# A decoder layer's expert stage: one-hots loaded once for each token, fewer tiles beside the selection

## The chip, the cores and the metric

The kernel runs on 1 core of one Trainium2 chip. The metric is the device time of one execution, in microseconds (us). The engines of a core each run their own list of instructions in order: PE (TensorE: matmuls; PEld is its weight loads), DVE (VectorE), ACT (ScalarE), POOL (GpSimd) and SP (SyncE, which here issues most transfers).

## The reference

One decoder layer for 256 tokens of width 1024: retention and attention heads between two projections, then a retrieval of single-neuron experts (PEER), then a norm. The change lies in the retrieval alone:

```python
def _peer(h, w_q, subkeys, w_down, w_up):      # 16384 experts, 8 heads, top 16, in blocks of 128 tokens
    q = (hblk @ w_q).reshape(B, TB, 8, 2, 128)
    s = einsum('btphd,phnd->btphn', q, subkeys)
    v, i = top_k(s, 16)                        # 16 of 128 for each half key
    cand = v[..., 0, :, None] + v[..., 1, None, :]
    cidx = i[..., 0, :, None] * 128 + i[..., 1, None, :]
    tv, tj = top_k(cand, 16)
    eidx = take_along_axis(cidx, tj, -1); w = softmax(tv)
    a = gelu(einsum('btd,btpkd->btpk', hblk, w_down[eidx]))
    return einsum('btpk,btpkd->btd', w * a, w_up[eidx])
```

## The kernel before

For 192 of the 256 tokens the experts aren't gathered: the hidden vectors are multiplied with all 16384 rows of `w_down` (128 **down units** of 128 experts, 512 KB each), gelu is taken, the result is multiplied by a weight matrix that is zero except at the chosen experts, and then multiplied with all of `w_up` (128 **up units**). For the other 64 tokens the chosen rows are gathered: 64 **sparse steps** for `w_down` (a gather of 512 KB on POOL, then a multiply with a sum on DVE: tile `row`, `dotS`) and 64 for `w_up` (`accS`).

A down unit comes in two forms. A *whole* unit multiplies the tile as loaded, in float32 (8 matmuls, each of which stands in the trace as two instructions of 192 columns: `acc<-h2f,raw`, `dn<-h2f,raw`). A *split* unit needs the tile cut into two fp32r parts (`H` on ACT, `L` on DVE, both 128x1024), takes 8 matmuls of 384 and 8 of 192 columns (`<-hT,H`, `<-hT,L`), and its two halves are added afterwards (`g` on ACT, then `g<-g,acc` on DVE). Up units are always split, and their gate values too (`a`).

The expert stage has three phases, kept by a loop over a list `seq` of units:

- **top**: after 16 query units, down units run on PE while DVE chooses the experts (`top_gen`, `top16`), for the first 128 tokens and then for the other 128. Each half ends with an exponential on ACT (`ex`, which needs an ACT table load before it and another after it), sums on DVE and three transposes on PE (`w<-ident,ef`, `w<-ident,ex`) that make the tables for the next phase. All down units of this phase are whole.
- **w**: `w_gen` builds the weight matrix in 48 groups of 4 tokens beside further down units. In a group DVE makes two one-hot tiles (`o1`, `o0`) and the high half of the weighted one-hot (`ow`), ACT the low half (`ow`, one instruction for each token), and PE multiplies them into one bank of PSUM: two loads of the same one-hot and two matmuls of 128 columns for each token. From the bank DVE multiplies into those parts of `VL`/`VH` whose down unit is already done, and ACT copies the others. Every third down unit is whole (`WD`).
- **up**: the remaining down units alternate with up units, then up units alone.

`credit` sets how many steps of `top_gen` or `w_gen` go with each unit: a unit adds `CT` in the phase top and `CD` in the phase w, and a step takes what it yields. `scred` does the same for sparse steps: `RD` for each unit, `RU` for each up unit. This list gives the order in which the instructions are written; a scheduler then orders them on DVE, ACT, PE and POOL, and `issue_after` keeps an instruction behind another one. SP issues loads in the written order. PSUM has 8 banks in this stage: 4 with the name `acc`, 2 `dn`, 2 `w`. Nearly all instructions of the trace carry line L88, a recording helper; so one goes by the tiles' names.

Of the kernel before, what the change touches and what calls it, by code (L numbers as in the profile page):

```python
# [24 lines left out]
F32 = mybir.dt.float32  # L25
# [11 lines left out]
P = 128  # L37
# [17 lines left out]
NJ = P // 2  # L55
BLK = 8
BD = 3
WD = 3
RD = 0.7
RU = 0.45  # L60
EARLY = 5
NF1 = 3
NF2 = 1
FAFTER = False
SPL = 1
CT = 1.1
AFTER = ("top",)
NCAND = 50
CAND = [(0, 0, 1, 16), (16, 1, 2, 8), (24, 2, 3, 5), (29, 3, 4, 4), (33, 4, 5, 3), (36, 5, 8, 2), (42, 8, 16, 1)]
# [2 lines left out]
def build(tc, I, out, dbg=None, stop=None):  # L72
# [868 lines left out]
    def top_gen(sc):  # L941

        for i in range(16):
            while i not in sc:
                yield None
            b = sc.pop(i)
            for tt in range(2):
                top16(b[:, tt, :], tv1[tt][:, i, :], ti1[tt][:, i, :], P, "s2")
                yield 1.1
        for tt in range(2):  # L950
            fi = mk(tk, (P, 8, 2, 16), F32, "fi", bufs=2)
            V.tensor_copy(fi, ti1[tt].rearrange("p (a b) c -> p a b c", b=2))
            V.tensor_scalar(fi[:, :, 0, :], fi[:, :, 0, :], 128.0, None, op0=ALU.mult)
            v4 = tv1[tt].rearrange("p (a b) c -> p a b c", b=2)
            cand = mk(tk, (P, 8, NCAND), F32, "cand", bufs=2)
            cidx = mk(tk, (P, 8, NCAND), F32, "cidx", bufs=2)
            for src, dst in ((v4, cand), (fi, cidx)):
                for o, a0, a1, nb in CAND:
                    n = (a1 - a0) * nb
                    V.tensor_tensor(dst[:, :, o:o + n].rearrange("p h (a b) -> p h a b", b=nb),  # L960
                                    src[:, :, 0, a0:a1, None].to_broadcast([P, 8, a1 - a0, nb]),
                                    src[:, :, 1, None, 0:nb].to_broadcast([P, 8, a1 - a0, nb]), op=ALU.add)
                yield 1.1
            tv = mk(tk, (P, 8, 16), F32, "tv", bufs=2)
            tp = mk(tk, (P, 8, 16), U32, "tp", bufs=2)
            tpf = mk(tk, (P, 8, 16), BF, "tpf", bufs=2)
            ev = mk(tk, (P, 8, 16), F32, "ev", bufs=2)
            for p in range(8):
                top16(cand[:, p, :], tv[:, p, :], tp[:, p, :], NCAND, "s3")
                V.tensor_copy(tpf[:, p, :], tp[:, p, :])  # L970
                oh = mk(tk, (P, NCAND, 16), BF, "oh", bufs=1)
                V.tensor_tensor(oh, ioj, tpf[:, p:p + 1, :].to_broadcast([P, NCAND, 16]), op=ALU.is_equal)
                oe = mk(tk, (P, NCAND, 16), F32, "oe", bufs=2)
                V.tensor_tensor(oe, oh, cidx[:, p, :, None].to_broadcast([P, NCAND, 16]), op=ALU.mult)
                V.tensor_reduce(ev[:, p, :], oe.rearrange("p j k -> p k j"), axis=AX.X, op=ALU.add)
                yield 2.1

            ex = mk(tk, (P, 8, 16), F32, "ex", bufs=2)
            V.tensor_tensor(ex, tv, tv[:, :, 0:1].to_broadcast([P, 8, 16]), op=ALU.subtract)
            S.activation(ex, ex, AF.Exp)  # L980
            sm = mk(tk, (P, 8), F32, "smx", bufs=2)
            V.tensor_reduce(sm, ex, axis=AX.X, op=ALU.add)
            V.reciprocal(sm, sm)
            V.tensor_tensor(ex, ex, sm[:, :, None].to_broadcast([P, 8, 16]), op=ALU.mult)
            ei = mk(tk, (P, P), I32, "ei", bufs=2)
            V.tensor_copy(ei, ev.rearrange("p a b -> p (a b)"))
            e1 = mk(tk, (P, 2, P), I32, "e1", bufs=1)
            V.tensor_scalar(e1[:, 0, :], ei, 7, None, op0=ALU.arith_shift_right)
            V.tensor_scalar(e1[:, 1, :], ei, 127, None, op0=ALU.bitwise_and)
            ef = mk(tk, (P, 2, P), F32, "ef", bufs=1)  # L990
            V.tensor_copy(ef, e1)
            if tt == 0:

                ew = ex.rearrange("p a b -> p (a b)")
                V.tensor_copy(idxS[:TS, :], ei[:TS, :NJ])
                V.tensor_copy(wS[:TS, :], ew[:TS, :NJ])
                G.dma_start(idxS[TS:, :], ei[:TS, NJ:])
                last["G"] = G.dma_start(wS[TS:, :], ew[:TS, NJ:])
                spg.append(sparse_gen())
            yield 1.3  # L1000
            b = bank("w")[:, :3 * P].rearrange("p (a b) -> p a b", a=3)
            PE.transpose(b[:, 0, :], ef[:, 0, :], ident)
            PE.transpose(b[:, 1, :], ef[:, 1, :], ident)
            PE.transpose(b[:, 2, :], ex.rearrange("p a b -> p (a b)"), ident)
            tq = slice(tt * P, (tt + 1) * P)
            S.activation(tab[:, :, tq], b[:, 0:2, :], AF.Copy)
            wt = mk(tk, (P, P), F32, "wt", bufs=1)
            S.activation(wt, b[:, 2, :], AF.Copy, scale=WSC)
            dump(f"e{tt}", ev)
            dump(f"w{tt}", ex)  # L1010

            V.tensor_copy(tabw[:, tq], wt)
            V.tensor_tensor(tabl[:, tq], wt, tabw[:, tq], op=ALU.subtract)
            yield 1.0
# [50 lines left out]
    def w_gen(ohp):  # L1065

        half = NT // 2
        for gi in range(TD // 4):
            v0 = gi * 4
            t0 = TS + v0  # L1070
            oh = []
            for n in (1, 0):
                o = mk(ohp, (P, P, WG), F16, f"o{n}")
                V.tensor_tensor(o, iow, tab[:, n, None, t0:t0 + WG].to_broadcast([P, P, WG]), op=ALU.is_equal)
                oh.append(o)
            ow = [mk(ohp, (P, P, WG), F16, f"ow{n}") for n in range(2)]
            V.tensor_tensor(ow[0], oh[1], tabw[:, None, t0:t0 + WG].to_broadcast([P, P, WG]), op=ALU.mult)
            for t in range(WG):
                S.activation(ow[1][:, :, t], oh[1][:, :, t], AF.Copy, scale=tabl[:, t0 + t:t0 + t + 1])
            b = bank("w").rearrange("p (a b) -> p a b", a=4)  # L1080
            for t in range(WG):
                for n in range(2):
                    mm(b[:, t, :], oh[0][:, :, t], ow[n][:, :, t], n == 0, n == 1)
            yield 1.0
            bv = b.rearrange("p t i -> p i t")
            na = state["na"]
            for i0, buf in ((0, VL), (half, VH[0])):
                a = min(max(na - i0, 0), half)
                o = buf[:, :, v0:v0 + 4]
                if a:  # L1090
                    V.scalar_tensor_tensor(o[:, :a, :], bv[:, i0:i0 + a, :], 1.0 / WSC, o[:, :a, :], op0=ALU.mult,
                                           op1=ALU.mult)
                if a < half:
                    S.activation(o[:, a:, :], bv[:, i0 + a:i0 + half, :], AF.Copy, scale=1.0 / WSC)
            state["t0"] = v0 + 4
            yield 0.4

    def down_unit(n):
        wide = n not in whole
        if wide:  # L1100
            h, l = splits.pop(("down", n))
        else:
            r, _ = raws.pop(("down", n))
        b = bank("dn" if phase == "up" or n % 3 == 2 else "acc")[:, :2 * TD]
        for k in range(KC):
            ks = slice(k * P, (k + 1) * P)
            if wide:
                two = [(b.rearrange("p (a b) -> p a b", a=2), h[:, ks], h2[k // 4][:, k % 4, :, TS:]),
                       (b[:, :TD], l[:, ks], h2H[:, k, TS:])]
                for n_, o in enumerate(two[::-1] if k else two):  # L1110
                    mm(*o, k == 0 and n_ == 0, k == KC - 1 and n_ == 1)
            else:
                mm(b[:, :TD], r[:, ks], h2f[:, k, :], k == 0, k == KC - 1)
        t0 = state["t0"]
        v = vtile(n)
        if t0 or wide:
            g = mk(gt, (P, TD), F32, "g")
        src = b
        if wide:
            S.activation(g, b[:, TD:], AF.Copy)  # L1120
            V.tensor_tensor(g, g, b[:, :TD], op=ALU.add)
            src = g
        if t0 < TD:
            last["U"] = S.activation(v[:, t0:], src[:, t0:TD], AF.Gelu_apprx_tanh)
        if t0:
            S.activation(g[:, :t0], src[:, :t0], AF.Gelu_apprx_tanh)
            last["U"] = V.tensor_tensor(v[:, :t0], v[:, :t0], g[:, :t0], op=ALU.mult)
        state["na"] = n + 1
# [100 lines left out]
    def split_to(i):  # L1229
        while splitted[0] <= i and splitted[0] < len(seq):  # L1230
            u, n = seq[splitted[0]]
            if u == "down" and (phase == "top" or phase == "w" and n % WD == 0):
                whole.add(n)
                splitted[0] += 1
                continue
# [245 lines left out]
```

## Time and profile before

| | us |
|---|---|
| median of 3 runs (966.09 to 971.69) | 967.46 |
| the profiled execution | 963.1 |
| its span | 960.9 |
| PE busy | 905.5 (94%) |
| DVE busy | 810.4 (84%) |
| ACT busy | 521.2 (54%) |
| POOL busy | 224.8 (23%) |

Matmuls overlap in the pipeline, so the busy time of PE says little of its speed; the distance from one unit's start to the next one's start does. In the program's span the first group of the phase w starts at 375.1 us, the last group ends at 570.0, the first up unit starts at 581.6, the last down unit at 682.1, and the last matmul ends at 948.2. The chain of waits lies 51% on PE, 26% on DVE, 8% on DMA and 7% on ACT.

### The profile page before, as it was taken

Reading aid. Unit: us, or ns where it says so; the run is one execution under the profiler, and the core shown is the slowest. Engines: PE = TensorE matmul, PEld = TensorE weight load, DVE = VectorE, ACT = ScalarE, POOL = GpSimd, SP = SyncE. Lnnn points to the kernel's source line nnn. Section 1 sums busy time; section 2 is a strip of 40 time slices with the busy share of each in tenths; the row PEclk is TensorE's granted clock in tenths of the full one; section 3 lists DMA queues with packets and bytes.
Section 4 is the critical chain, followed back from the end, with each engine's and each line's share of the span. In section 5 each row is a group of like instructions: output and inputs, shape, how many; then the busy total and the mean of one; then the engine's idle time right before and its main releaser. Section 6 shows DMA issues by size and latency. Waiting matters only on the chain.

```text
span 960.9 us, 15265 instructions
## 1 busy us (share of the span) xinstructions
PE 905.5 (94%) x5198; PEld 797.2 (83%) x5198; DVE 810.4 (84%) x1788; ACT 521.2 (54%) x1151; POOL 224.8 (23%) x172
## 2 busy tenths in 40 slices
PE   7999999999999799999989987899999989999994
PEld 6875667899999799999989986788887867888883
DVE  7988888689998922899998986889988979898887
ACT  7543697344221123778776754556564545555564
POOL 2040000110004200123223312334442425233311
PEclk9999999999999899999999988999999999999998
DMA  9978765354569976778777677899999999899981
GB/s 361 393 283 290 263 220 177 129 158 143 153 207 387 338 227 218 260 264 281 270 257 263 248 255 258 288 321 345 348 351 359 384 352 354 339 337 341 332 290 44
DMA packets 74749, 266.43 MB, mean 277 GB/s; under 512 B 9400, under 2 KB 9712, under 8 KB 74288
## 3 DMA queue, kind: packets, MB, share of 16 engines
q1 hardware_dynamic: 55200, 193.59, 57.5%
q0 software_dynamic: 19328, 71.61, 20.4%
q8 instruction: 41, 0.67, 0.3%
q14 instruction: 36, 0.29, 0.1%
q10 hardware_dynamic: 144, 0.26, 0.1%
HBM read 263.03 MB, written 2.11 MB: 276 GB/s over the span
## 4 chain that ended last, share of the span: by engine, by line
PE 51%; DVE 26%; DMA 8%; ACT 7%; issue 6%; POOL 1%; SPq 0%; DVEq 0%; ACTq 0%; POOLq 0%
PE acc L88 32%; DVE row L88 5%; PE C L88 5%; PE dn L88 4%; PE O L88 4%; DVE L L88 4%; PE S L88 3%; PE T L88 2%; DVE ev L88 2%; DVE o L88 2%; DMA row<-in_downN_dram,idxS 2%; ACT H L88 2%; ACT ow L88 1%; DMA raw<-in_down_dram 1%; DVE VL L88 1%
## 5 line engine op out<-in xcount | busy, mean ns | idle before, releaser
L88 DVE TENSOR_TENSOR L<-raw,H 128x1024 fp32r<-128x1024 f32 x216 | 263.2, 1220 | 41.9 <-ACT H L88 37.3
L88 ACT ACTIVATE H<-raw 128x1024 fp32r<-128x1024 f32 x216 | 228.2, 1058 | 122.2 <-DMA raw<-in_up_dram 73.4
L88 PE MATMUL acc<-H,a 128*128 128x512 f32 (+1 forms) x774 | 269.9, 397 | 4.4 <-DVE a L88 4.3
L88 PE MATMUL acc<-L,a 128*128 128x512 f32 (+1 forms) x515 | 203.4, 395 | 6.7 <-DVE L L88 6.7
L88 PEld LDWEIGHTS acc<-H,a 128*128 128x128 f32 x774 | 149.4, 193 | 39.8 <-DVE a L88 9.6
L1025 POOL DMA_INDIRECT row<-in_up_dram,idxS x64 | 116.2, 1815 | 196.2 <-DVE accS L88 163.8
L88 PE MATMUL acc<-h2f,raw 128*128 128x192 f32 x816 | 139.2, 326 | 0.0
L1025 POOL DMA_INDIRECT row<-in_downN_dram,idxS x64 | 77.5, 1210 | 242.6 <-DVE VH L88 85.4
L88 PEld LDWEIGHTS acc<-h2f,raw 128*128 128x128 f32 x816 | 133.0, 190 | 0.0
L88 PEld LDWEIGHTS acc<-L,a 128*128 128x128 f32 x515 | 99.1, 192 | 26.5 <-DVE L L88 7.1
L88 PE MATMUL dn<-hT,H 128*128 128x384 f32 x328 | 101.8, 367 | 5.4 <-DVE g L88 5.2
L88 PE MATMUL acc<-hT,H 128*128 128x256 f32 (+1 forms) x408 | 98.0, 323 | 3.6 <-ACT g L88 3.6
L88 DVE SCALAR_TENSOR_TENSOR row<-row,h2rep 128x1024 f32<-128x1024 f32 x64 | 77.9, 1218 | 8.8 <-DMA row<-in_downN_dram,idxS 8.6
L88 DVE SCALAR_TENSOR_TENSOR accS<-row,cS,accS 128x1024 f32<-128x1024 f32 x64 | 81.7, 1277 | 2.2 <-DMA row<-in_up_dram,idxS 2.2
L88 PE MATMUL dn<-hT,L 128*128 128x192 f32 x328 | 77.1, 255 | 0.0
L88 ACT ACTIVATE ow<-o,VL 128x128 f16<-128x128 f16 x192 | 74.4, 572 | 4.0 <-DVE o L88 3.4
L88 PEld LDWEIGHTS acc<-hT,H 128*128 128x128 f32 x408 | 69.7, 194 | 3.9 <-ACT g L88 3.9
L88 PE MATMUL acc<-hT,L 128*128 128x192 f32 (+1 forms) x280 | 72.5, 270 | 0.0
L88 PEld LDWEIGHTS dn<-hT,H 128*128 128x128 f32 x328 | 62.5, 191 | 8.5 <-DVE g L88 7.3
L88 PEld LDWEIGHTS dn<-hT,L 128*128 128x128 f32 x328 | 62.8, 193 | 0.7
L88 PE MATMUL w<-ow,o 128*128 128x128 f16 x384 | 53.2, 296 | 4.1 <-DVE ow L88 2.5
L88 PE MATMUL dn<-h2f,raw 128*128 128x192 f32 x272 | 48.5, 333 | 6.3 <-ACT VL L88 6.3
(355 smaller groups left out, 1367.2 us busy)
## 6 DMA issues: line engine op xcount, KB each, us to landing
raw<-in_down_dram SPq DMA_DIRECT2D x128, 512.0 KB, 4.3
raw<-in_up_dram SPq DMA_DIRECT2D x128, 512.0 KB, 6.3
adaraw<-in_wadaT_dram SPq DMA_DIRECT2D x40, 512.0 KB, 6.0
raw<-in_wq_dram SPq DMA_DIRECT2D x16, 512.0 KB, 3.5
raw<-in_win_C_dram SPq DMA_DIRECT2D x12, 512.0 KB, 6.3
rawA<-in_win_A_dram SPq DMA_DIRECT2D x8, 512.0 KB, 6.5
raw<-in_wout_dram SPq DMA_DIRECT2D x8, 512.0 KB, 3.7
VL<-in_wadaT_dram SPq DMA_DIRECT2D x8, 512.0 KB, 7.1
```

Source lines behind the costliest of these rows:

```text
L88: i = fn(*a, **kw)
L1025: G.indirect_dma_start(r, None, src, bass.IndirectOffsetOnAxis(ap=idxS[:, j:j + 1], axis=0))
```

## The change

- `w_gen`: the two weighted one-hots of a token lie side by side in one tile `ow`, so that one load of `o1` and one matmul of 256 columns serve a token. Their results no longer add up in PSUM: they stand beside each other, and a group takes two banks `w`. ACT copies one half, scaled, into a tile `wl` (one buffer), DVE adds the other half to it, and the multiplication and the copy into `VL`/`VH` read `wl`.
- `split_to`: all down units of the phase w are whole, and in the phase up those of odd number. A whole unit there goes to a bank `dn`, a split one to a bank `w`.
- `CT` goes from 1.1 to 1.5, `RD` from 0.7 to 0.9, `RU` from 0.45 to 0.3. Counted from the loop: the phase top has 35 down units in place of 47, the phase w 58 in both, the phase up 35 in place of 23. In all 111 down units are whole (68 before) and 17 are split (60 before). Of the sparse steps, 14, 52 and 63 stand in the three phases (15, 40 and 74 before).
- The exponential is kept behind the last gelu that was written before it.

```diff
-WD = 3
-RD = 0.7
-RU = 0.45
+RD = 0.9
+RU = 0.3
-CT = 1.1
+CT = 1.5
...
-            S.activation(ex, ex, AF.Exp)
+            with (tc.issue_after(last["U"].ins) if "U" in last else ExitStack()):
+                S.activation(ex, ex, AF.Exp)
...
-            ow = [mk(ohp, (P, P, WG), F16, f"ow{n}") for n in range(2)]
-            V.tensor_tensor(ow[0], oh[1], tabw[:, None, t0:t0 + WG].to_broadcast([P, P, WG]), op=ALU.mult)
+            ow = mk(ohp, (P, 2, P, WG), F16, "ow")
+            V.tensor_tensor(ow[:, 0], oh[1], tabw[:, None, t0:t0 + WG].to_broadcast([P, P, WG]), op=ALU.mult)
             for t in range(WG):
-                S.activation(ow[1][:, :, t], oh[1][:, :, t], AF.Copy, scale=tabl[:, t0 + t:t0 + t + 1])
-            b = bank("w").rearrange("p (a b) -> p a b", a=4)
-            for t in range(WG):
-                for n in range(2):
-                    mm(b[:, t, :], oh[0][:, :, t], ow[n][:, :, t], n == 0, n == 1)
+                S.activation(ow[:, 1, :, t], oh[1][:, :, t], AF.Copy, scale=tabl[:, t0 + t:t0 + t + 1])
+            bs = []
+            for t in range(0, WG, 2):
+                b = bank("w").rearrange("p (t n i) -> p t n i", t=2, n=2)
+                for q in range(2):
+                    mm(b[:, q], oh[0][:, :, t + q], ow[:, :, :, t + q], True, True)
+                bs.append(b)
             yield 1.0
-            bv = b.rearrange("p t i -> p i t")
+            wl = mk(ohp, (P, WG, P), F32, "wl", bufs=1)
+            for t, b in enumerate(bs):
+                x = wl[:, 2 * t:2 * t + 2, :]
+                S.activation(x, b[:, :, 1, :], AF.Copy, scale=1.0 / WSC)
+                V.scalar_tensor_tensor(x, b[:, :, 0, :], 1.0 / WSC, x, op0=ALU.mult, op1=ALU.add)
+            bv = wl.rearrange("p t i -> p i t")
...
-                    V.scalar_tensor_tensor(o[:, :a, :], bv[:, i0:i0 + a, :], 1.0 / WSC, o[:, :a, :], op0=ALU.mult,
-                                           op1=ALU.mult)
+                    V.tensor_tensor(o[:, :a, :], bv[:, i0:i0 + a, :], o[:, :a, :], op=ALU.mult)
                 if a < half:
-                    S.activation(o[:, a:, :], bv[:, i0 + a:i0 + half, :], AF.Copy, scale=1.0 / WSC)
+                    S.activation(o[:, a:, :], bv[:, i0 + a:i0 + half, :], AF.Copy)
...
-        b = bank("dn" if phase == "up" or n % 3 == 2 else "acc")[:, :2 * TD]
+        b = bank(("dn" if n % 2 else "w") if phase == "up" else "dn" if n % 3 == 2 else "acc")[:, :2 * TD]
...
-            if u == "down" and (phase == "top" or phase == "w" and n % WD == 0):
+            if u == "down" and (phase != "up" or n % 2):
```

PE where the phase top passes into the phase w, before: the last whole down units (`<-h2f,raw`), the three transposes, one more unit, the first group. This is the 46th down unit in the first row.

```order
L88 MATMUL acc_3672<-h2f_1960,raw_3590 128x192 x8
L88 MATMUL w_3685<-ident_66,ef_3668 128x128 x2
L88 MATMUL w_3685<-ident_66,ex_3656 128x128
L88 MATMUL acc_3696<-h2f_1960,raw_3602 128x192 x8
L88 LDWEIGHTS o_801_3717
L88 MATMUL w_3728<-ow_803_3721,o_801_3717 128x128
L88 LDWEIGHTS o_801_3717
L88 MATMUL w_3728<-ow_804_3722,o_801_3717 128x128
```

The same place after, where the first row is the 34th down unit, and `w_3580`, `w_3583` are the group's two banks.

```order
L87 MATMUL acc_3525<-h2f_1960,raw_3423 128x192 x8
L87 MATMUL w_3538<-ident_66,ef_3521 128x128 x2
L87 MATMUL w_3538<-ident_66,ex_3509 128x128
L87 MATMUL acc_3549<-h2f_1960,raw_3452 128x192 x8
L87 LDWEIGHTS o_776_3570
L87 MATMUL w_3580<-ow_3574,o_776_3570 128x256
L87 LDWEIGHTS o_776_3570
L87 MATMUL w_3580<-ow_3574,o_776_3570 128x256
L87 LDWEIGHTS o_776_3570
L87 MATMUL w_3583<-ow_3574,o_776_3570 128x256
```

Twelve down units fewer stand ahead of the transposes, and a token's two loads and two matmuls are one of each.

DVE at the end of the choice of experts for the second half of the tokens, before; `ex` is the exponential's result, `ef` the chosen experts' numbers, `o` a one-hot of a group.

```order
L88 TENSOR_REDUCE smx_3659<-ex_3656 128x8
L88 CAST ei_3663<-ev_3347 128x128
L88 RECIPROCAL smx_3659<-smx_3659 128x8
L88 TENSOR_SCALAR e_790_3665<-ei_3663 128x128
L88 TENSOR_TENSOR ex_3656<-ex_3656,smx_3659 128x128
L88 TENSOR_SCALAR e_790_3665<-ei_3663 128x128
L88 SCALAR_TENSOR_TENSOR row_3615,dotS_2001<-row_3615,h2rep_1938 128x1024
L88 CAST ef_3668<-e_790_3665 128x256
```

And after:

```order
L87 CAST ef_3521<-e_765_3518 128x256
L87 TENSOR_TENSOR o_783_3596<-VL_1982 128x512
L87 TENSOR_TENSOR o_797_3656<-VL_1982 128x512
L87 TENSOR_TENSOR ow_3598<-o_783_3596,VL_1982 128x512
L87 TENSOR_TENSOR o_807_3700<-VL_1982 128x512
L87 TENSOR_TENSOR cS_2002<-cS_2002,wS_2000 128x8
L87 TENSOR_REDUCE smx_3512<-ex_3509 128x8
L87 RECIPROCAL smx_3512<-smx_3512 128x8
L87 TENSOR_TENSOR ex_3509<-ex_3509,smx_3512 128x128
```

One-hots of the first groups now stand ahead of the last sum `ex`, which the third transpose reads; three more of them stand ahead of `ef`.

DVE in the middle of the phase w, before: one group and the work up to the next one's evacuation.

```order
L88 SCALAR_TENSOR_TENSOR VL_1982<-w_4758,VL_1982 128x64x4
L88 TENSOR_TENSOR o_1029_4850<-VL_1982 128x512
L88 TENSOR_TENSOR ow_1031_4854<-o_1030_4852,VL_1982 128x512
L88 TENSOR_TENSOR o_1055_4979<-VL_1982 128x512
L88 TENSOR_TENSOR g_4790<-g_4790,acc_4773 128x192
L88 SCALAR_TENSOR_TENSOR VL_1982<-w_4813,VL_1982 128x64x4
L88 TENSOR_TENSOR o_1046_4929<-VL_1982 128x512
L88 TENSOR_TENSOR L_4900<-raw_4767,H_4899 128x1024
L88 TENSOR_TENSOR VH_3713<-VH_3713,g_4790 128x76
L88 SCALAR_TENSOR_TENSOR row_4617,dotS_2001<-row_4617,h2rep_1938 128x1024
```

And after:

```order
L87 SCALAR_TENSOR_TENSOR wl_4184<-w_4160,wl_4184 128x256
L87 SCALAR_TENSOR_TENSOR wl_4184<-w_4163,wl_4184 128x256
L87 TENSOR_TENSOR o_932_4234<-VL_1982 128x512
L87 TENSOR_TENSOR ow_4238<-o_933_4236,VL_1982 128x512
L87 TENSOR_TENSOR o_957_4338<-VL_1982 128x512
L87 TENSOR_TENSOR VL_1982<-VL_1982,g_4177 128x52
L87 SCALAR_TENSOR_TENSOR row_4039,dotS_2001<-row_4039,h2rep_1938 128x1024
L87 TENSOR_TENSOR VL_1982<-wl_4184,VL_1982 128x51x4
```

The splits `L` and the adds `g` are gone from this stretch; two adds into `wl` stand there for each group, and every group is followed by a sparse step.

## Rows read from the trace of the kernel before

**Rows 1.** The page's first line.

```profile
span 960.9 us, 15265 instructions
```

**Rows 2.** Windows: stretch; busy PE, PEld, DVE, ACT, POOL; clock, DMA share, GB/s.

```profile
244.00:375.10 131.10, 124.83 (x763) 124.47 (x762) 94.27 (x333) 25.70 (x68) 22.06 (x22) 0.97 0.76 260
375.10:574.60 199.50, 191.57 (x1330) 186.28 (x1328) 181.11 (x437) 148.44 (x445) 48.97 (x39) 0.97 0.77 262
574.60:592.90 18.30, 11.59 (x61) 10.35 (x61) 12.68 (x23) 5.97 (x15) 6.75 (x5) 0.82 0.66 212
592.90:684.50 91.60, 86.42 (x486) 77.46 (x485) 80.43 (x117) 53.16 (x93) 30.85 (x18) 1.00 0.91 321
684.50:818.40 133.90, 129.51 (x543) 103.49 (x541) 117.98 (x154) 72.19 (x109) 54.61 (x30) 0.99 0.96 362
818.40:946.50 128.10, 128.10 (x556) 105.34 (x555) 110.14 (x137) 74.85 (x112) 34.68 (x22) 1.00 0.84 302
```

**Rows 3.** PE's timeline, end of top: start us, us, instruction, count, idle before.

```profile
334.26 4.30 PE L88 MATMUL dn<-h2f,raw 128*128 128x192 f32 x16 [6.27 <-ACT VL L88]
...
372.20 0.38 PE L88 MATMUL w<-ident,ef 128*128 128x128 f32 x2
...
372.52 2.77 PE L88 MATMUL acc<-h2f,raw 128*128 128x192 f32 x16
375.13 1.11 PE L88 MATMUL w<-ow,o 128*128 128x128 f16 x8
```

**Rows 4.** DVE's timeline at the same place.

```profile
335.17 1.22 DVE L88 SCALAR_TENSOR_TENSOR row<-row,h2rep 128x1024 f32<-128x1024 f32 x1
...
336.31 0.29 DVE L88 CAST ef<-e 128x256 f32<-128x256 int32 x1
...
341.48 0.43 DVE L88 TENSOR_TENSOR o<-VL 128x512 f16<-128x512 f16 x1 [0.95 <-ACT ow L88]
...
373.31 0.23 DVE L88 CAST VL<-wt 128x128 f16<-128x128 f32 x1 [21.09 <-ACT wt L88]
```

**Rows 5.** ACT's timeline at the second exponential.

```profile
330.96 1.28 ACT L88 ACT_TABLE_LOAD   x1 [21.14 <-DVE ex L88]
```

**Rows 6.** PE's timeline in the phase w.

```profile
445.36 1.11 PE L88 MATMUL w<-ow,o 128*128 128x128 f16 x8
446.29 2.78 PE L88 MATMUL acc<-h2f,raw 128*128 128x192 f32 x16
448.91 1.11 PE L88 MATMUL w<-ow,o 128*128 128x128 f16 x8
449.77 0.42 PE L88 MATMUL acc<-hT,H 128*128 128x384 f32 x1
...
452.14 1.11 PE L88 MATMUL w<-ow,o 128*128 128x128 f16 x8
```

**Rows 7.** DVE's groups from 375 to 575: count, busy us, mean ns, idle before.

```profile
L88 DVE TENSOR_TENSOR L<-raw,H 128x1024 fp32r<-128x1024 f32 x41 | 50.0, 1218 | 4.7 <-ACT H L88 4.6
L88 DVE SCALAR_TENSOR_TENSOR row<-row,h2rep 128x1024 f32<-128x1024 f32 x39 | 47.5, 1217 | 0.0
...
L88 DVE SCALAR_TENSOR_TENSOR VL<-w,VL 128x256 f32<-128x256 f32 x35 | 14.5, 416 | 0.2 <-PE w L88 0.2
...
L88 DVE TENSOR_TENSOR g<-g,acc 128x192 f32<-128x192 f32 x19 | 6.6, 346 | 3.5 <-ACT g L88 3.5
```

**Rows 8.** PE's timeline in the phase up: a split unit, an up unit, the next.

```profile
597.59 0.34 PE L88 MATMUL dn<-hT,H 128*128 128x384 f32 x1
...
599.86 0.39 PE L88 MATMUL acc<-H,a 128*128 128x512 f32 x1
...
602.17 0.34 PE L88 MATMUL dn<-hT,H 128*128 128x384 f32 x1
```

**Rows 9.** PE's longest wait at the start of the phase up.

```profile
588.71 0.80 PE L88 MATMUL acc<-L,a 128*128 128x512 f32 x1 [6.71 <-DVE L L88]
```

**Rows 10.** DVE's timeline just before it.

```profile
584.87 1.23 DVE L88 SCALAR_TENSOR_TENSOR row<-row,h2rep 128x1024 f32<-128x1024 f32 x1 [4.18 <-DMA row<-in_downN_dram,idxS]
```

## The prediction

> **What bounds the kernel now.** I read the page first, for the span [rows 1], then the windows of the expert stage, cut where PE's timeline changes its kind of work [rows 2]. The reader is to see there that PE is busy in nearly every stretch, but that DVE is close behind from 375 to 684, and that the transfers run at a share of 0.96 from 684 to 818. So no engine has much room, and the time is PE's work plus the gaps that others force on it. Then PE's timeline at the end of the phase top [rows 3] and DVE's and ACT's beside it [rows 4, 5]: DVE has finished choosing at 336.6 and its next work of any weight starts at 373, with a wait of 21.09 us, because PE still has down units to do ahead of the second transposes at 372.20. In this stretch PE alone is the limit. Last, the distances from start to start in PE's timeline, which price a unit [rows 6, 8].
>
> PE's prices are these. Whole unit: 446.29 to 448.91, 2.62 us. Group: 0.93 and 0.86, taken as 0.90. Split unit: 449.77 to 452.14, 2.37 in the phase w [rows 6], and 597.59 to 599.86, 2.27 in the phase up; up unit 2.31 [rows 8]. From the first group at 375.1 to 946.5, 571.4 us, the work is 21 whole units (55.0), 38 and 22 split ones (90.1 and 49.9), 48 groups (43.2) and 128 up units (295.7), together 533.9. The other 37.5 us are gaps: by the windows [rows 2] 11.2 up to 574.6 (199.5 less 188.3), 9.2 up to 592.9 (18.3 less three split units and one up unit), 4.6 up to 684.5 (91.6 less 19 of each), and 12.5 from there on (262.0 less 108 up units), of which 8.8 lie before 818 (543 matmuls at the pace of the later window, 128.1 / 556, make 125.1 of 133.9).
>
> **The change, part by part.** The sum is made against the profiled execution, 963.1 us with a span of 960.9; that lies 4.4 below the median of the runs, and I carry the difference over unchanged.
>
> *Fewer units beside the choice.* Twelve whole units leave PE's list ahead of the second transposes. Without the wait of 6.27 us and the slow unit behind it (4.30 in place of 2.77) [rows 3] and without twelve times 2.61 (372.52 to 375.13), PE is there at 372.2 - 31.3 - 7.8 = 333.1. What is late next is DVE. Its `ef` ended at 336.6 [rows 4]. One sparse step fewer lies ahead of it (-1.2), but seven one-hot tiles of the first groups, some 0.34 us each, now stand ahead of `ex` (+2.4), and the three small steps that make `ex` come last (+0.8): 338.6. PE then waits 5.5 us, does the transposes, the 35th unit (2.6, and 1.5 more if it runs slowly as after the 6.27 us) and starts the first group at 343. That is 32.1 us sooner. The bounds are 336, if DVE is not late, and 350, if the one-hots wait for ACT.
>
> *The exponential behind the last gelu.* ACT stood 21.14 us for DVE's `ex` [rows 5] with gelus queued behind it, PE ran out of banks and waited 6.27 us [rows 3]. That wait is the one I removed above, so it isn't counted again. The new rule puts the exponential behind the gelu of the 33rd unit, at about 330 of the old time, where DVE's `ex` is ready anyway; cost nothing, covered by DVE's own work up to 336. If DVE were sooner, two table loads of 1.28 each would show.
>
> *No splits in the phase w, half of them in the phase up.* Of the 93 down units that follow the first group 76 are whole and 17 split, where it was 21 and 60 of 81. On PE that is 199.1 + 38.6 = 237.7 in place of 195.0, so 42.7 more; twelve of these units come from the phase top. DVE loses 38 splits and 38 adds in the phase w, 38 x (1.22 + 0.35) = 59.4 us [rows 7].
>
> *One load for each token.* A group is 4 loads and 4 matmuls of 256 columns in place of 8 and 8 of 128. The trace has no such matmul. If the load sets the pace, as it may for 0.90 / 8 = 0.11 a pair now, a group takes 0.45. If load and columns add up, with 128 columns at 0.058 (2.31 / 10 for 512), it is 4 x (0.055 + 0.115) = 0.68. The nearest row is the split unit, eight pairs of together 576 columns in 2.27, or 0.49 ns a column: 4 x 256 x 0.49 = 0.51, which I take. The 48 groups fall from 43.2 to 24.5.
>
> That loads run beside matmuls is seen in the window from 818 to 946, where PE is busy 128.10 of 128.10 us and PEld 105.34 of them [rows 2]. [...]
>
> DVE pays for the merged matmul: two adds for each group, 96 of the size of the old multiplication out of PSUM, 0.416 each, 39.9 us [rows 7]; the multiplication itself then reads `wl` and is taken as equally long. With 12 more sparse steps of 1.22 (14.6) DVE in the phase w stands at -59.4 + 39.9 + 14.6 = -4.9 of its 181.1 us [rows 2]. PE there has 58 x 2.62 + 24.5 = 176.5 in place of 188.3 with one whole unit more. Both fall, by a little, and DVE stays close to PE; so I leave the gaps of this phase at 11.2. ACT does 38 fewer `H` and 96 more copies out of PSUM and has room (148 of 199.5).
>
> *Moved sparse steps and more pairs in the phase up.* 63 steps stand there in place of 74. The waits at its start, 6.71 us on PE for a split [rows 9], behind a DVE that waited 4.18 for a gathered row [rows 10], have nothing in the change that takes them away: 9.2 stays. In the pairs DVE goes down from 3.2 + 1.15 steps to 2.5 + 1.2 steps for each pair on average, while PE's pair gets longer (4.58 to 4.77): 4.6 becomes 2. Up units alone come with 0.3 steps in place of 0.45, and so with less to transfer in the stretch whose DMA share is 0.96: 12.5 becomes 7. The bounds are 0 and the old 26.3 for all three; 18.2 is what I take, 8.1 less. POOL's gathers go with the steps; the small copy of the weights (`wS`) now waits behind eleven of them, and only the sparse weights read it, later.
>
> The sum: start of the groups -32.1; units +42.7; groups -18.7; gaps -8.1: -16.2 us, or 946.9 for the profiled execution and **951 us** beside the runs' median.
>
> **The rivals.**
> *The evacuation becomes the wait (slower).* Both banks `w` now belong to one group, and the next group may only start when DVE's second add has read them; before, the other bank was free. For it: DVE is in order, busy 181 of 199.5 us, and each group is followed by a sparse step of 1.22. Against it: a whole unit of 2.62 lies between two groups nearly everywhere, and the adds stand at once behind ACT's copies. If one group in two pays a sparse step, it is 24 x 1.22 = 29: 980 us. It decides from 16.2 / 48 = 0.34 us a group on.
> *The time is only moved (no change).* The twelve units and the longer units come back in full after the first group, and the gaps of the phase up stay at 26.3 since 353 GB/s in the pairs (3.2 tiles of 0.524 MB in 4.75 us) is no less than the 321 to 362 now [rows 2]: 951 + 8 and 3 more for a later first group, 962 us.
> *The relief of DVE and ACT is worth more.* Without splits a down unit waits only for its transfer: half of the 11.2 goes, 4 us at the start of the phase up, and groups at the load's pace (-3): 938 us.
>
> **How the numbers follow.** My forecast 0.58; evacuation 0.12; only moved 0.15; more relief 0.15. What a measurement can tell from no change is about 0.5%, 4.8 us, so from 962.6 to 972.3. Faster: 0.95 of the forecast, all of the relief and a third of the moved time, 0.75. Within 0.5%: 0.13. Slower: the evacuation, 0.12. The range goes from the relief's 938 to 967, past the third case; the slow case and the rims of the first are left out, about 0.2.
>
> **What would show it.** The first group at about 343 and PE's wait ahead of the second transposes near 5 us, with no wait of PE for ACT's `VL` near 330. Groups 0.45 to 0.68 us apart from the next unit. From the first group to the end about 587 us (571.4 + 15.9). Wrong would be: waits of PE's `w` for DVE's `wl` of more than 0.3 us a group; a first group after 350; gaps behind it of 37 us or more.

## The result, and the profile after

The changed kernel takes 980.0 us (median of 4 runs, 974.8 to 983.7) against 968.8 for the kernel before beside it: a ratio of 1.0114, interval 1.0073 to 1.0155. It is slower, and I had forecast 951, faster, with 967 as the upper end. The prediction was wrong in sign and outside its range.

The span of its profiled execution is 978.8 us, against 960.9 [rows 1]. The windows of its expert stage, cut at the first group, the last group, some 5 us behind the first up unit, the last down unit and the first matmul of the final rows; columns as in [rows 2], which cut a little otherwise:

```profile
243.60:357.68 114.08, 93.79 (x571) 93.17 (x570) 92.71 (x330) 22.77 (x56) 21.51 (x20) 0.91 0.70 235
357.68:548.09 190.41, 190.25 (x1092) 171.64 (x1091) 174.73 (x460) 146.87 (x469) 47.44 (x49) 1.00 0.86 288
548.09:567.59 19.50, 17.25 (x104) 16.15 (x103) 15.45 (x26) 8.08 (x19) 5.90 (x5) 0.99 0.95 346
567.59:727.21 159.62, 150.44 (x797) 135.53 (x798) 119.16 (x159) 69.98 (x123) 55.12 (x39) 0.98 0.91 323
727.21:962.19 234.98, 226.86 (x962) 184.82 (x962) 179.33 (x237) 128.80 (x197) 36.82 (x23) 0.99 0.81 284
```

Two things stand out. The phase top has a hole: PE is busy for only 93.79 of 114.08 us. And the phase w has none, 190.25 of 190.41, so that what it lasts is PE's own work. From the last group to the final rows PE does wait; its two largest waits there, with total, times and longest:

```profile
PE dn L87 <- DVE g L87: 10.1, 7, 2.3
PE acc L87 <- DVE a L87: 8.1, 5, 4.3
```

PE's timeline of the changed kernel: the first half's transposes, the second half's, and two groups in the middle of the phase w. It answers to [rows 3, 6].

```profile
295.87 0.38 PE L87 MATMUL w<-ident,ef 128*128 128x128 f32 x2
296.09 2.12 PE L87 MATMUL dn<-h2f,raw 128*128 128x192 f32 x12
318.39 0.48 PE L87 MATMUL w<-ident,ex 128*128 128x128 f32 x1 [20.18 <-DVE ex L87]
...
354.41 0.38 PE L87 MATMUL w<-ident,ef 128*128 128x128 f32 x2
354.90 0.33 PE L87 MATMUL w<-ident,ex 128*128 128x128 f32 x1
...
357.68 1.08 PE L87 MATMUL w<-ow,o 128*128 128x256 f16 x4
...
401.57 1.07 PE L87 MATMUL w<-ow,o 128*128 128x256 f16 x4
402.46 2.78 PE L87 MATMUL acc<-h2f,raw 128*128 128x192 f32 x16
405.08 1.08 PE L87 MATMUL w<-ow,o 128*128 128x256 f16 x4
```

PE stood 20.18 us for the third transpose of the *first* half of the tokens, a place of which the prediction says nothing. The first group came at 357.68, 17.5 sooner than the 375.13 of before, not 32.1. And a group still takes 0.89 us (401.57 to 402.46), with half of the instructions.

ACT's timeline and then DVE's, where the first half's exponential stands:

```profile
293.82 1.28 ACT L87 ACT_TABLE_LOAD   x1
295.12 0.31 ACT L87 ACTIVATE ex<-ex 128x128 f32<-128x128 f32 x1
```

```profile
314.95 0.56 DVE L87 TENSOR_TENSOR oh<-VL,tpf 128x800 bf16<-128x800 bf16 x1
315.43 0.28 DVE L87 TENSOR_REDUCE smx<-ex 128x8 f32<-128x128 f32 x1
...
318.05 0.28 DVE L87 TENSOR_TENSOR ex<-ex,smx 128x128 f32<-128x128 f32 x1
```

The exponential was done at 295.43. DVE came to its sum only at 315.43, in the middle of the second half's choice (`oh`, `oe`, `ev`). In these 20 us DVE waited 1.8 us for gathered rows; the rest is work that stood ahead of the sum in DVE's order of instructions. DVE's groups in the phase w, to be held against [rows 7], show what the relief was spent on:

```profile
L87 DVE SCALAR_TENSOR_TENSOR row<-row,h2rep 128x1024 f32<-128x1024 f32 x50 | 60.9, 1219 | 0.0
...
L87 DVE SCALAR_TENSOR_TENSOR wl<-w,wl 128x256 f32<-128x256 f32 x94 | 35.8, 418 | 1.9 <-ACT wl L87 0.8 <-issue 0.8
...
L87 DVE TENSOR_TENSOR VL<-wl,VL 128x256 f32<-128x256 f32 x23 | 14.0, 611 | 0.0
```

The `L` and `g` are gone, the adds into `wl` cost what I took (418 for 416 ns). The multiplication out of `wl`, which I had taken as equally long, takes 611 ns and not the 416 of the old one out of PSUM. That costs PE nothing here: in the whole phase w PE waited once, 0.2 us for `ow`, and DVE has 15.7 us free.

### The profile page after: what moved, and what is told of

Its sections match the earlier page's. It is cut to its first block, busy times and chain, and to the rows that moved or that the text cites. A ratio compares the mean times of both kernels' runs of the same rounds, so it can differ in the third digit from the quotient of the medians.

```text
span 978.8 us, 14840 instructions
## 1 busy us (share of the span) xinstructions
PE 914.4 (93%) x5004; PEld 793.0 (81%) x5006; DVE 795.9 (81%) x1800; ACT 518.1 (53%) x1172; POOL 193.7 (20%) x172
## 4 chain that ended last, share of the span: by engine, by line
PE 59%; DVE 19%; DMA 14%; issue 4%; ACT 3%; POOL 1%; SPq 0%; DVEq 0%; ACTq 0%; POOLq 0%
PE acc L87 32%; PE dn L87 8%; DMA raw<-in_up_dram 7%; PE w L87 5%; PE C L87 5%; DVE L L87 4%; PE O L87 3%; DMA raw<-in_down_dram 2%; PE S L87 2%; PE T L87 2%; DVE ti L87 2%; DVE ev L87 2%; DVE tv L87 2%; DMA VL<-in_wadaT_dram 1%; DMA VL<-csd 1%
## 5 line engine op out<-in xcount | busy, mean ns | idle before, releaser
L87 DVE TENSOR_TENSOR L<-raw,H 128x1024 fp32r<-128x1024 f32 x173 | 211.1, 1222 | 84.4 <-ACT H L87 56.5
L87 ACT ACTIVATE H<-raw 128x1024 fp32r<-128x1024 f32 x173 | 182.6, 1058 | 182.9 <-PE acc L87 81.2
L87 PE MATMUL dn<-h2f,raw 128*128 128x192 f32 x784 | 140.7, 333 | 10.1 <-DVE g L87 10.1
L87 PEld LDWEIGHTS dn<-h2f,raw 128*128 128x128 f32 x784 | 132.7, 194 | 16.6 <-DVE g L87 13.2
L87 PE MATMUL w<-ow,o 128*128 128x256 f16 x192 | 52.8, 403 | 0.2 <-DVE ow L87 0.2
L87 DVE SCALAR_TENSOR_TENSOR adaraw<-adaraw,cs 128x1024 f32<-128x1024 f32 x40 | 48.5, 1217 | 0.0
L87 PE MATMUL acc<-hT,H 128*128 128x256 f32 x256 | 47.8, 287 | 0.0
L87 DVE TENSOR_TENSOR o<-VL 128x512 f16<-128x512 f16 x96 | 39.2, 417 | 4.7 <-PE w L87 2.4
L87 PE MATMUL C<-H,hT 128*128 128x512 f32 (+1 forms) x128 | 41.9, 389 | 0.3 <-ACT xT L87 0.2
L87 PE MATMUL w<-hT,H 128*128 128x384 f32 x136 | 41.3, 359 | 0.3 <-ACT g L87 0.3
```

Of the source, the lines that this page charges most:

```text
L87: i = fn(*a, **kw)
```

## The experiments

All times are medians; a ratio is that to the kernel before beside the same runs (966.3, 965.7, 967.1 and 965.9 us in the four series).

**The kept-back exponentials.** Two runs, the rule on the second half alone, and on none.

```diff
-            with (tc.issue_after(last["U"].ins) if "U" in last else ExitStack()):
+            with (tc.issue_after(last["U"].ins) if tt else ExitStack()):     # second half only; or no rule at all
```

> The changed kernel, but the first half's exponential is no longer kept behind the last gelu (the second half's still is). Theory: PE's 20.2 us wait ahead of the third transpose of the first half (318.39) comes from that rule alone; it goes, PE then waits some 4 us for DVE's `ef` of the second half (338.5), the first group starts at 341 to 344 in place of 357.7, and the time is 964 to 967 in place of 980. Rival: the second half's choice on DVE holds the first group in any case, the wait only moves: first group at 355 or later, 977 to 982.

> The changed kernel with both exponentials free, as in the kernel before. Theory: as with the first one free (first group 341 to 344, 964 to 967), since the wait of ACT for DVE's `ex` of the second half (21.1 us before) costs PE some 6 us for banks only in time in which it would wait for DVE's `ef` anyway. Rival: these 6 us come on top, first group at 348 to 350, 970 to 973.

Measured: 968.0 us (1.0012, 0.9979 to 1.0044) and 964.5 us (0.9974, 0.9936 to 1.0013). PE's timeline and a row of ACT's with the rule on the second half:

```profile
340.98 0.69 PE L87 MATMUL w<-ident,ef 128*128 128x128 f32 x2 [7.63 <-ACT VL L87]
346.57 0.48 PE L87 MATMUL w<-ident,ex 128*128 128x128 f32 x1 [4.90 <-DVE ex L87]
346.84 4.18 PE L87 MATMUL acc<-h2f,raw 128*128 128x192 f32 x16
350.86 1.07 PE L87 MATMUL w<-ow,o 128*128 128x256 f16 x4
```

```profile
339.59 1.18 ACT L87 ACTIVATE ow<-o,VL 128x128 f16<-128x128 f16 x3 [26.68 <-DVE o L87]
```

And PE's timeline and a row of DVE's with no rule:

```profile
332.20 5.49 PE L87 MATMUL dn<-h2f,raw 128*128 128x192 f32 x16 [5.47 <-ACT VL L87]
...
340.54 0.38 PE L87 MATMUL w<-ident,ef 128*128 128x128 f32 x2
...
343.47 1.08 PE L87 MATMUL w<-ow,o 128*128 128x256 f16 x4
```

```profile
335.18 0.29 DVE L87 CAST ef<-e 128x256 f32<-128x256 int32 x1
```

With no rule at all the theory's numbers hold: 15.5 us are gone by the medians (13.5 by the ratios), the 20 us wait is gone, and the first group starts at 343.47, where the forecast had 343. The waits are not those that I had named. PE waited 5.47 us for ACT's `VL`, that is for a bank of PSUM, and the two units behind that wait took 8.3 us and not 5.2; DVE's `ef` was done at 335.5, 5 us before PE came to the transposes.

With the rule on the second half alone 12 us are gone (9.9 by the ratios), and the time is 1 us above my range. My figure for the first group (341 to 344) was missed: it came at 350.86. ACT stood 26.68 us for a one-hot `o` with gelus behind it in its list, so PE waited 7.63 us for a bank; the exponential stood behind these gelus, and PE waited 4.90 us more for `ex`. So the rule costs at both places; in the changed kernel the first hid the second.

**The same rule on the kernel before**, whose phase top has twelve units more:

> The kernel before with only the two exponentials kept behind the last gelu written ahead of them. Theory: the price is not in the exponential's time on ACT but in DVE's written order, which puts the first half's `smx`, `ex` behind the second half's choice: PE waits for `ex` at its third transpose from 314.7 to some 335 us here too, and gets 6 to 8 us back as ACT no longer stands 21 us for the second `ex`: first group at 385 to 392, time 976 to 984. Rival: twelve more units on PE cover it: first group at 366 to 376, time 957 to 967.

Measured: 985.5 us, 1.0195 (1.0167 to 1.0224). PE's timeline:

```profile
313.04 0.38 PE L88 MATMUL w<-ident,ef 128*128 128x128 f32 x2
334.26 0.47 PE L88 MATMUL w<-ident,ex 128*128 128x128 f32 x1 [20.84 <-DVE ex L88]
```

The wait is there with all 47 units, as PE works its list in order and the transpose stands ahead of the second half's units. The first group starts at 389.8: the mechanism was right, the time 1.5 us above my bound.

**What a group costs.** First the columns of `ow` side by side, and the groups of the kernel before:

```diff
-            ow = mk(ohp, (P, 2, P, WG), F16, "ow")          # columns of a token 4 elements (8 bytes) apart
+            ow = mk(ohp, (P, WG, 2, P), F16, "ow")          # first run: side by side
...
+            (second run: w_gen as in the kernel before, one bank, 8 loads and 8 matmuls)
```

> The changed kernel with `ow` kept as [token, half, 128], so that the 256 columns of a token's matmul lie side by side and not 8 bytes apart; DVE and ACT write it with the same number of elements, DVE with a stride. Theory: PE reads 16-bit columns that lie 8 bytes apart at about half the pace, so a group falls from 0.90 to 0.45 to 0.55 us; PE in the phase w falls by 17 to 21 of 190 us, DVE (174.7 busy, more if its strided write is slower than 0.41 us) then becomes the limit, and the time is 962 to 975. Rival: the price hangs on loads or on columns whatever their distance, the group stays at 0.90, 979 to 984.

> The changed kernel with the groups of the kernel before: two loads and two matmuls of 128 columns for a token, one bank, no `wl`. Theory: PE's price of a group is 0.90 us in both forms, so PE and the time stay (977 to 983), while DVE loses some 45 us of its 175 in the phase w. Rival: the single load is worth what I forecast, 0.4 us a group, and the time rises by 15 to 19 to 995 to 999.

Measured: 1039.3 us (1.0736, 1.0645 to 1.0826) and 975.3 us (1.0089, 1.0050 to 1.0128). The first run's time missed both theories, because of DVE; PE's timeline and DVE's groups (358 to 624) of it:

```profile
459.66 0.63 PE L87 MATMUL w<-ow,o 128*128 128x256 f16 x4 [1.63 <-DVE ow L87]
460.12 2.12 PE L87 MATMUL dn<-h2f,raw 128*128 128x192 f32 x12
```

```profile
L87 DVE TENSOR_TENSOR ow<-o,VL 128x512 f16<-128x512 f16 x46 | 111.8, 2431 | 0.1
```

DVE's write of `ow` with a distance of 512 bytes from element to element took 2.43 us in place of 0.42, and DVE (258.95 of 263.20 us) set the pace. But on PE the group took 0.46 us (459.66 to 460.12), and that tells the theories apart. In the second run PE was busy for 190.91 us in the phase w against 190.25, so the merge saved PE nothing. Its time is 4.7 us below the changed kernel's and 1.7 below my range, but the intervals of the two ratios overlap; that the merge costs time is not shown by this pair.

**Columns 4 bytes apart**, in tiles that DVE can write in the order in which they lie, with free exponentials:

```diff
-                o = mk(ohp, (P, P, WG), F16, f"o{n}")
+                o = mk(ohp, (P, 2, P, 2), F16, f"o{n}")        # [pair of tokens, 128, 2]
-            ow = mk(ohp, (P, 2, P, WG), F16, "ow")
+            ow = mk(ohp, (P, 2, 2, P, 2), F16, "ow")
...
+                    mm(b[:, r], oh[0][:, q, :, r], ow[:, :, q, :, r], True, True)
```

> The changed kernel with both exponentials free, and the one-hots `o`, `ow` and their index table kept as [pair of tokens, 128, 2] in place of [128, 4]: a token's columns lie 4 bytes apart and not 8, and DVE still writes whole tiles in the order in which they lie. Theory: at 4 bytes a column PE reads at its full pace (a 4-byte fp32r operand of 512 columns takes 0.23 us a matmul), the group falls from 0.90 to 0.46 us as with columns side by side, `ow` on DVE stays at 0.41 us, PE's work in the phase w falls from 190 to some 170, DVE (175) becomes its limit, and the time is 945 to 953 against 964.5 with the exponentials free alone. Rival: any distance halves the pace: group 0.90, 961 to 968.

Measured: 951.0 us, 0.9842 (0.9798 to 0.9886), as the theory has it. PE's timeline, in the phase w and then beside up units:

```profile
432.29 0.62 PE L87 MATMUL w<-ow,o 128*128 128x256 f16 x4
432.75 2.76 PE L87 MATMUL dn<-h2f,raw 128*128 128x192 f32 x16
...
560.01 2.87 PE L87 MATMUL dn<-h2f,raw 128*128 128x192 f32 x16
562.58 0.52 PE L87 MATMUL acc<-H,a 128*128 128x512 f32 x1
562.94 0.39 PE L87 MATMUL acc<-L,a 128*128 128x512 f32 x1
563.17 0.40 PE L87 MATMUL acc<-H,a 128*128 128x512 f32 x1
...
565.03 0.34 PE L87 MATMUL w<-hT,H 128*128 128x384 f32 x1
```

The group is 0.46 us at a distance of 4 bytes, and DVE's `ow` stays at 416 ns. The window of the phase w:

```profile
342.20:516.95 174.75, 169.49 (x1094) 161.56 (x1092) 169.77 (x457) 136.06 (x469) 46.81 (x49) 1.00 0.88 314
```

It is 15.6 us shorter than the 190.38 with the exponentials free alone, of the 21 that the groups lose on PE; 4.6 of the 5.3 us in which PE now idles are waits for DVE's `ow`. Is the single load needed for it? The same layout with two loads, one bank and no `wl`:

> The run with free exponentials and plain groups (963.4), with the one-hots in the pair layout (columns 4 bytes apart) but still two loads and two matmuls of 128 columns a token. Theory: with the columns at full pace a matmul of 128 would take 0.057 us, but the weight load (0.11 us from one to the next at best) then sets the pace, so the group stays at 0.85 to 0.92 and the time at 959 to 967; the single load is needed as well as the distance. Rival: the distance was the whole price, the group falls to 0.45 to 0.55, PE's work in the phase w to some 171 us with DVE at 141, and the time to 940 to 947.

Measured: 946.9 us, 0.9791 (0.9741 to 0.9841). My theory fell. PE's timeline:

```profile
422.69 0.62 PE L87 MATMUL w<-ow,o 128*128 128x128 f16 x8
423.15 2.82 PE L87 MATMUL acc<-h2f,raw 128*128 128x192 f32 x16
```

Eight loads and eight matmuls take 0.46 us too. The merge had no gain on PE to give, in either layout; it only cost DVE and ACT their work on `wl`. The phase w lasts 171.7 us without that work and 174.75 with it; the 4 us between the two times are within the scatter of four runs each.

**The exponentials free and plain groups**, **the counts alone** on the kernel before, and **every third unit of the phase w split** on the first of these:

> The changed kernel with both exponentials free and with the groups of the kernel before (two loads, two matmuls a token, no `wl`). Theory: the two losses are independent; first group at 343, the phase w 190.9 us long, and the time 957 to 963. Rival: without the adds DVE reaches other work earlier and the gain of the free exponential is partly the same microseconds: 963 to 970.

> The kernel before with only the three counts changed (CT 1.5, RD 0.9, RU 0.3): the phase top has 35 down units, the splits, the groups and the free exponential are as before. Theory: DVE becomes the limit of the phase w, with 140.7 us in it as in the changed kernel with plain groups and 38 splits and adds of together 1.57, 200 us for 58 units where PE needs 184; first group at 343, phase w 198 to 206, time 958 to 968. Rival: PE's prices alone decide, whole units cost their 0.25 us more than split ones and nothing else does: phase w 184 to 187, time 943 to 950.

> The changed kernel with both exponentials free, plain groups as before, and every third down unit of the phase w split again (19 or 20 of 58). Theory: PE gains 0.25 us for each split unit, 4.8, and DVE with 140.7 + 30 of some 186 us still has room: phase w 186 to 188, time 952 to 959. Rival: the waits for `L` and `g` give the gain back: phase w 190 or more, 958 to 965.

Measured: 963.4 us (0.9984, 0.9962 to 1.0006), 972.2 us (1.0077, 1.0052 to 1.0103), 959.5 us (0.9916, 0.9895 to 0.9937). The first lies at the border of its two theories; its phase w lasted 190.9 us, as forecast, its first group came at 345.7, and beside 964.5 with the merge it says once more that the merge gains nothing. In the second the phase w lasted 201.1 us, within the theory's range, but no engine fills it (PE busy 187.3, DVE 185.3; PE's longest waits are 6.4 us for DVE's `ow` and 6.0 for ACT's `g`), and the time was 4 us above the range: the three counts alone, with all the splits kept, make the kernel slower. In the third the phase w lasted 186.8 us, as forecast, but its time lies where the two theories meet, and its runs (955.7 to 969.4) overlap those of the first.

**What the splits cost.** The merged pair layout alone and the two-load pair layout alone on the kernel before; then on the run of 946.9: all units of the phase up split, with that every third of the phase w, and the first of these with the old counts. All units of the phase up split were also tried on the run of 951.0.

```diff
-            if u == "down" and (phase != "up" or n % 2):
+            if u == "down" and phase != "up":                                    # up all split
+            if u == "down" and (phase == "top" or phase == "w" and n % 3):       # and a third of w
```

> The kernel before with only its groups changed to one load and one matmul a token, in the pair layout with `wl`. Theory: PE loses 21 of 195 us in the phase w, but DVE gets 49 us more on top of 177 and sets the pace there, 215 to 228 us, so the kernel becomes slower, 982 to 1000: the merge pays only where splits are taken away. Rival: DVE's work hides, the 21 us come in full: 943 to 950.

> The kernel before with only the pair layout of the one-hots. Theory: PE's work in the phase w falls by 21 of 195 us (48 groups from 0.90 to 0.46), but DVE is busy there for 177 us and becomes the limit: phase w 180 to 187 us, time 954 to 960; the rest can only be had where splits are taken away. Rival: all of it is had, phase w 174, time 944 to 950.

> The run with free exponentials and the pair layout (951.0), with all 35 down units of the phase up split in place of every second one. Theory: some 17 units become 0.3 us shorter on PE, 5 us, and DVE (119.7 of 163 us between the first up unit and the last down unit) has room for 17 more `L` and `g` of together 1.57: 944 to 949. Rival: the pairs wait for transfers and for `L` in any case, and the 27 us more on DVE come ahead of the `a` that up units need: 950 to 958.

> Free exponentials, pair layout with two loads and no `wl` (946.9), and all 35 down units of the phase up split. Theory: the 11.7 us that this rule gave beside the merged groups (951.0 to 939.2) lie in the phase up and are independent of the groups: 933 to 938. Rival: without the DVE work of the phase w the sparse steps arrive otherwise and the pairs wait for transfers: 939 to 944.

> As the run beside it, and every third down unit of the phase w split as well. Theory: PE gains 0.25 us for each of 19 or 20 units, 5 us, and DVE has 139 + 30 of 167 us and is just full: 928 to 934. Rival: DVE sets the pace of the phase w now, its gaps take the 5 us back: 934 to 941.

> As the run with all units of the phase up split, with the counts of the kernel before (CT 1.1, RD 0.7, RU 0.45): 47 down units beside the choice, 35 behind the phase w again 23. Theory: the twelve units were only moved, 32 us sooner for 12 x 2.4 behind, and the counts are worth 3 us or less beside a free exponential: 935 to 942. Rival: the units beside the choice cost more than their time, as ACT stands for the exponential and PE for banks (6.3 us): 943 to 950.

| run | us | ratio | phase w |
|---|---|---|---|
| before, pair layout merged | 997.3 | 1.0309 (1.0285 to 1.0332) | 226.6 |
| before, pair layout, two loads | 968.2 | 0.9998 (0.9968 to 1.0029) | 192.0 |
| merged pairs (951.0), up all split | 939.2 | 0.9720 (0.9683 to 0.9756) | 174.7 |
| two-load pairs (946.9), up all split | **936.7** | 0.9699 (0.9665 to 0.9734) | 171.7 |
| the same, a third of w split | 951.1 | 0.9859 (0.9817 to 0.9902) | 181.0 |
| up all split, old counts | 946.1 | 0.9785 (0.9742 to 0.9828) | 174.8 |

The theories of the first and the fourth row hold; the third run is faster than I expected, and the second and the fifth missed both of their theories. The windows of the phase w, as above: the kernel before, that kernel with the two-load layout, the 936.7 run, that run with a third split, and the run of 959.5, which has a third split beside groups of 0.90 us.

```profile
375.13:570.02 194.89, 186.96 (x1298) 181.70 (x1297) 176.81 (x427) 145.67 (x437) 47.92 (x38) 0.97 0.78 265
```

```profile
380.39:572.41 192.02, 173.48 (x1298) 165.03 (x1297) 176.43 (x427) 137.94 (x437) 47.52 (x38) 0.97 0.78 267
```

```profile
343.41:515.10 171.69, 171.55 (x1282) 167.53 (x1281) 138.64 (x364) 99.16 (x373) 46.27 (x49) 1.00 0.92 319
```

```profile
344.36:525.35 180.99, 170.78 (x1283) 164.99 (x1281) 160.26 (x401) 117.29 (x408) 52.34 (x49) 0.98 0.87 305
```

```profile
344.25:531.09 186.84, 185.87 (x1283) 181.69 (x1281) 162.66 (x401) 129.13 (x408) 52.23 (x49) 1.00 0.85 296
```

In the kernel before, the cheap groups (0.46 us) shorten PE's busy time by 13.5 us, the phase by only 2.9 and the kernel not at all: PE idles for 18.5 us where it idled for 7.9. I had expected half of the gain. The last row of the table is this kernel with the splits of the phase w taken out as well, and the banks of the phase up chosen by the unit's number: 946.1 against 968.2, with a phase w that is 17.2 us shorter. So with cheap groups taking the splits out of the phase w was right.

Putting a third of them back says the same. PE idles for 10.2 us where it idled for none, and the run is 14.4 us slower, where I had expected 5 faster. The two longest of its waits in the phase w:

```profile
PE dn L87 <- ACT g L87: 3.8, 2, 2.9
PE w L87 <- DVE ow L87: 3.3, 4, 1.0
```

Beside the groups of 0.90 us the same third left PE idle for only 1.0 us of 186.84. DVE's busy share does not tell the two apart (87% there, 89% here), so why the waits come in one and not in the other stays open.

In the phase up the reverse holds: the half-split rule cost 11.7 us (951.0 to 939.2), or 10.2 on the other base (946.9 to 936.7). On the merged pairs, from 5 us behind the first up unit to the last down unit, first half and then all split:

```profile
536.48:699.76 163.28, 152.20 (x797) 137.38 (x798) 119.66 (x159) 70.25 (x124) 52.44 (x39) 0.97 0.88 313
```

```profile
535.65:688.58 152.93, 143.56 (x795) 128.59 (x794) 140.39 (x190) 88.04 (x152) 63.40 (x40) 0.99 0.94 336
```

Most of it is PE's own time, 8.6 us less; DVE has the room, 140 of 153.

The counts are worth 9.4 us (946.1 to 936.7), three times what I allowed: the run with the old ones misses its theory and meets the rival's time. Of the rival's reason 4.2 us show: with the new counts the first group comes 35.5 us sooner (343.41 for 378.92), where twelve units are 31.3. PE's longest waits in the phase w of the first row of the table:

```profile
PE w L88 <- DVE wl L88: 18.4, 8, 6.7
PE dn L88 <- DVE wl L88: 8.9, 5, 5.3
```

That is the wait for the evacuation which I had as a rival, at a place where the splits are still there (DVE busy for 215 of 227 us).

## Why the prediction was wrong, step by step

- **The exponential, "cost nothing": failed, 14 to 15 us.** The step says that the rule "puts the exponential behind the gelu of the 33rd unit" and that it is covered by DVE's work. The rule acts on both halves, and I priced the second alone. In the changed kernel DVE's order has `smx` and `ex` of the first half among the second half's choice, and the transpose that reads them stands in PE's list ahead of some 13 units (318.65 to 354.41). The price of the second half was wrong too: with the rule there alone the first group came 7.4 us later than with none (350.86, 343.47).
- **Fewer units beside the choice, first group at 343: the number came without the rule, by luck.** I had taken off the wait for banks with its slow unit (7.8 us) and put in a wait for DVE (5.5 us) and a slow unit (1.5). Without the rule the wait for a bank was there (5.47 us and slow units behind it), and DVE, which was to be "late next", was done 5 us before PE came. (Ahead of `ex` stood eight one-hot tiles, not seven, which changes this by 0.3 us.) The errors cancel; what is left is the twelve units, 31.3 of the 31.7 us by which the first group is sooner (375.13 to 343.47).
- **One load for each token, -18.7: failed, nothing came.** I took three readings of 0.90 us (load, load plus columns, columns of another operand) and none by the address. The price was the distance of the columns. With them 4 bytes apart the group is 0.46, near the 0.51 taken, and then the number of loads does not matter.
- **Units +42.7 and gaps -8.1: right together.** From the first group to the first matmul of the final rows it is 604.5 us (357.68 to 962.19) against 569.55 before (375.13 to 944.68), 35.0 more where the two terms make 34.6. How the 35.0 is shared between them goes by the forecast's prices, of which the whole unit's is met (402.46 to 405.08, 2.62).
- **The gaps in their two parts: both wrong.** By these prices the phase w had 11.6 us of gaps between its first and last group (194.9 less 20 whole units, 37 split ones and 48 groups, 183.3) and now has 0.5 (190.4 less 56 whole units and 48 groups, 189.9); I had left them all. From there on it had 24.2 (374.7 less 350.5) and has 27.4 (414.1 less 386.7), where I had taken 8.1 off; the waits for DVE's `g` and `a`, together 18.2 us, are most of it. A whole unit between up units also costs a little more than its 2.62: with the up unit behind it, it took 5.02 us (560.01 to 565.03 in the run of 951.0) and not 4.93, as the first matmul behind it takes 0.36 us to the next and not 0.23 (562.58, 562.94, 563.17 above).
- **The evacuation rival: its time came (980), its wait did not.** PE waited 0.2 us in the whole phase w. A time that fits a rival is no proof of it; the rival was priced at one group in two.

The two failed terms are 14.6 (32.1 less 17.5) and 18.7 us, and 951 + 33.3 is 984, 4 above what was measured. With the rule taken out and the columns 4 bytes apart, and the rest of the change as it was, the kernel takes 951.0, the number that the prediction gave for it. That is in part luck: the first group's figure and the gaps each held errors of opposite sign, and the cheaper groups gave 13.5 us of time (964.5 to 951.0) and not 18.7.

## What to carry to other kernels

Where a rule keeps an instruction back, look in every engine's list for each place at which it acts, and ask there not whether the kept-back engine has time, but where its reader's reader stands in line. Before an operation is priced by its number of loads and columns, write down the address step of each operand: a layout that is free for one engine may halve the pace of another (DVE wrote `ow` in 0.417 us with columns 8 bytes apart and in 0.416 with 4, and PE took 0.89 and 0.46 us for a group), and a one-time price from a row is only good for that step. Whether a form that is cheaper on a busy engine (split units on PE) is worth taking is read from the waits of a run, not from the busy share of the engines that pay for it: with the same third of units split, DVE was busy for 87% and for 89% of the phase w, and PE idled for 1.0 and for 10.2 us.

## What the runs showed of the hardware

- TensorE read a 16-bit moving operand with columns 8 bytes apart at half the pace: four matmuls of 256 columns in 0.89 us, against 0.46 with columns 4 bytes apart and 0.46 with columns side by side.
- Eight loads of 128 columns with eight matmuls of 128 took 0.46 us, 0.058 for each pair, at a distance of 4 bytes, and four loads with four matmuls of 256 took the same; at 8 bytes it was 0.90 and 0.89. Half the loads made no difference in either layout.
- VectorE wrote a 16-bit tile of 512 elements in 2.43 us with a distance of 512 bytes and in 0.42 in order.
- VectorE's multiplication by a tile read in another order than it lies took 611 ns out of SBUF (`tensor_tensor`) and 416 out of PSUM (`scalar_tensor_tensor`), for the same 256 elements; whether the memory or the instruction makes the difference no run shows.
